# Experts' stage of a layer kernel: three buffers for the weight loads, the first product by halves, and the low part of U on VectorE

## The chip, the cores and the metric

The kernel runs on one core of a Trainium2 chip, in one launch. The metric is the device time of one execution in microseconds (us), less is better. Engines are named as the profile names them: PE (TensorE, matmuls), PEld (its weight loads), DVE (VectorE), ACT (ScalarE), POOL (GpSimd), SP (SyncE, which only issues DMAs here). SPq is the queue of SP.

## The reference

One layer on 1024 tokens of 1024 channels: a mixer sublayer (state-space scan and convolution, joined by an output projection), then a retrieval sublayer, and a last norm. The change lies in the retrieval sublayer. Every token chooses, for each of 8 heads, the 16 best of 16384 experts; an expert is a row of `u_tab` and a row of `v_tab`:

```python
def block(args):
    xb, eb, gb = args
    act = jax.nn.gelu(jnp.einsum("pd,ped->pe", xb, u_tab[eb]), approximate=False)
    return jnp.einsum("pe,ped->pd", gb * act, v_tab[eb])
...
x = x + mod[:, 5, None, :] * peer(modulate(rms_norm(x, norm2_w[i]), ...), ...)
...
return rms_norm(x, final_norm_w)
```

All of it is float32. A product that must be exact to float32 is made of three: each operand is split into a high part (a copy in the type fp32r) and a low part (the rest), and low x high, high x low and high x high are summed.

## The kernel before, in words

Tokens come in 8 blocks of 128. Before the experts' stage the kernel has normed the tokens (`h2T`, channels on partitions), chosen the experts of the first seven blocks and, for the first five (`ND`), written a matrix of gates to DRAM (`g_dram`). The experts' stage does two things side by side.

**The dense blocks.** For the first five blocks all 16384 experts are computed, 128 at a time, with TensorE. `In` (one object per 128 experts, 128 in all) is the first product: `load` brings 128 columns of U (512 KB, tile `u`) and, for every second object, a tile of gates `gm`; `split` makes the high part `uh` (ACT) and the low part `ul` (POOL) of U by `hi_lo`; `mm` calls `multiply_u`, 48 matmuls of 320 columns into two PSUM tiles `pa` (one per half of the 640 tokens; the pool has three); `post` applies the activation into `ga` (ACT); `weigh` multiplies `ga` by the gates (DVE) and makes the high part `wh` (ACT); `low` makes the low part `wl` (DVE). `Out` (256 objects) is half of the columns of the second product for 128 experts: `load` brings 128 x 512 of V (256 KB, tile `v`), `split` makes `vh` (ACT) and `vl` (DVE), `mm` issues 15 matmuls of 512 columns into five PSUM tiles `pv`, which sum over a group of 8 experts' blocks; `sum` adds them to the output in `h2T` (DVE) at the end of a group.

**The gathered blocks.** For the last three blocks the rows of U and V that each token chose are gathered: `gathered()` yields one step per row and token block. A step issues an indirect DMA of 512 KB on POOL's queue (`ask`, tile `gr`, a ring of `NGB` = 5 buffers, three asked ahead) and runs one multiply-and-sum on DVE (`scalar_tensor_tensor`). `finish(z, a)` is the end of such a block: the residual and the last norm, with loads of `x1_dram` and of a gate row into tiles of the same ring. `h2`, the tokens of a gathered block, is reloaded between blocks. `advance` interleaves these steps with the dense work: about 2.8 steps in each `In.mm` and 1.7 in each `Out.mm`, counted by `IN_US` and `OUT_US`. The choice of the last block's experts (`choosing`) is interleaved in the same place during the first groups.

**The order.** `seq` lists the objects: 8 In, then for each group 8 Out of the first columns, one In of the next group, 8 Out of the second columns, seven In. Each engine runs its instructions in the order in which the loop at the end emits them, and a queue of DMAs stops at a DMA that has to wait for its buffer. The loop emits, for object n: the load of object n+2, the split of object n+1, `weigh` of the object before if it was an In, the product of n with its share of gather steps, `low` of the object before, and `post` of n:

```python
for n, x in enumerate(seq):
    if n + 2 < len(seq):
        seq[n + 2].load()
    if n + 1 < len(seq):
        seq[n + 1].split()
    before = seq[n - 1] if n and isinstance(seq[n - 1], In) else None
    if before:
        before.weigh()
    x.mm()
    if before:
        before.low()
    x.post()
```

The tiles `u`, `uh`, `ul`, `v`, `vh`, `vl` and `gm` have two buffers each. In the last group `post` of the first Out objects also loads the residual and scales the sums (POOL), for the last norm of the dense blocks. The rows of the trace name the lines: L60 is the low part made by `hi_lo`, L59 its high part; L985 the first product; L1415 to L1417 the second; L1275 the gather; L1297 and L1309 the gathered multiply-and-sums with U and with V; L1380 the activation, L1384 `weigh`, L1386 `wh`, L1390 `wl`, L1401 V's load, L971 U's.

Of the kernel before, what the change touches and what calls it, by code (L numbers as in the profile page):

```python
# [18 lines left out]
P = 128  # L19
# [18 lines left out]
ND = 5                   # token blocks whose experts go through dense products; the others gather theirs  # L38
TD = ND * P
TH = TD // 2  # L40
NS = 7                   # token blocks whose experts are chosen before the products
NGB = 5                  # rows of gathered experts on chip
IN_US, OUT_US = 18, 11    # shares of the gather steps beside 128 experts' first product and half of their second
GE = 8                   # blocks of 128 experts between two sums into the output

# The pairs of ranks (i, j) that can be among the top ones: (i + 1)(j + 1) <= 16; those of the upper half have
# (i + 1)(j + 1) <= 8. Pieces are (i0, i1, j0, j1); sums stand in lexicographic order, numbers of experts with the first 20 ahead.
# [15 lines left out]
def mm3(nc, out, a, b, n, start=True, stop=True):  # L63
    """out += sum_k a[k].T @ b[k] in float32 accuracy; a, b give (hi, lo) pairs of a k."""
# [7 lines left out]
def layer_kernel(ctx, tc, A, dbg=None):  # L72
# [8 lines left out]
    # ------------------------------------------------------------------ constants  # L81
# [9 lines left out]
    def rsqrt(dst, src, scale, n):  # L91
        """dst = 1 / sqrt(src * scale + eps) on a small tile, with one Newton step."""
# [15 lines left out]
    row_dram = dram.tile([1, D], F32, name="row_dram")          # gate of the second sublayer  # L108
# [3 lines left out]
    g_dram = dram.tile([ND, 2, P, P, P // 2], F32, name="g_dram")   # gates: [token block, half, second key, first key, token]  # L112
# [32 lines left out]
    # chunks of w_in_t: 0-3 z, 4-7 x, 8-9 B, 10-11 C, 12-15 GLU value, 16-19 GLU gate, 20 dt  # L145
# [14 lines left out]
    def modulate(j):  # L160
        """h1 of the tokens or of the context in [channel, token] layout, split."""
# [9 lines left out]
    # ------------------------------------------------------------------ modulation, norm 1  # L171
    with ExitStack() as st:
# [22 lines left out]
        # sums of squares of the tokens from the transposed tensors  # L195
# [17 lines left out]
        # rows of scale and shift for both conditions, then as columns  # L213
# [747 lines left out]
    mix.close()  # L961
    dbg("h2T", h2T)

    # ------------------------------------------------------------------ what the dense experts need first
    late = ExitStack()
    e1 = e2 = hh2 = hl2 = None
    U = {}
# [599 lines left out]
```

## Time and profile before

| | |
|---|---|
| median of 3 runs | 3207.91 us (3204.24 to 3208.45) |
| profiled execution, span from the first to the last instruction | 3212.8 us |
| PE busy | 2880.9 us, 90% of the span |
| DVE busy | 2693.3 us, 84% |
| POOL busy | 2002.0 us, 62% |
| ACT busy | 1002.9 us, 31% |
| gathers, queue q0 | 402.70 MB, 35.5% of the 16 DMA engines' time |
| other loads, queue q1 | 315.72 MB, 28.6% |

The profiled execution's own time is its span; no time outside the span is given for it. The profile is that of one execution on the chip: busy time is the time in which an engine ran an instruction, idle time before an instruction is put down to what ended it ("<-"). In groups of instructions a mean is that of one instruction in ns. Names are the program's tiles, out<-in. The matrix engine's matmuls are pipelined: the time from one start to the next is what one costs.

### The profile page before, as it was taken

The page shows a single profiled execution, that of the slowest core. Times are in us where ns is not written, and L with a number is a line of the kernel's source. Part 1 is how long each engine was busy: PE and PEld are TensorE (multiplying, and loading weights), DVE is VectorE, ACT ScalarE, POOL GpSimd, SP SyncE. Part 2 cuts the span into 40 slices and gives each one's busy share as a digit, 9 for nine tenths or more (in the row PEclk, how much of TensorE's full clock was granted, in tenths as well). Part 3 has the DMA queues.
Part 4 walks back from the last instruction along what each step waited for, and adds up shares of the span by engine and source line. Part 5 has one row for each costly group of instructions (what it writes and reads, how often), then busy time and mean ns, then how long its engine had stood idle before and what let it go on. Part 6 is the DMA issues. An engine that isn't in the chain of part 4 may idle for free.

```text
span 3212.8 us, 41810 instructions
## 1 busy us (share of the span) xinstructions
PE 2880.9 (90%) x14905; PEld 2383.1 (74%) x14905; DVE 2693.3 (84%) x4828; ACT 1002.9 (31%) x1584; POOL 2002.0 (62%) x1478
## 2 busy tenths in 40 slices
PE   7999777998888768988999999999999899999996
PEld 4777676754555558877788788888888788888884
DVE  5897888559999997889898887888898888888896
ACT  3224323324555552322222222222222222222222
POOL 0222455316666777777677676776687677777773
PEclk8999998999999879999999999999999999999998
DMA  6111454341212237877888888899889889889883
GB/s 203 59 40 40 127 160 147 99 164 60 85 80 105 105 125 264 314 262 268 298 276 306 303 303 309 315 313 323 302 310 325 303 299 331 308 303 319 303 312 109
DMA packets 334113, 721.09 MB, mean 224 GB/s; under 512 B 24512, under 2 KB 167120, under 8 KB 332624
## 3 DMA queue, kind: packets, MB, share of 16 engines
q0 software_dynamic: 110592, 402.70, 35.5%
q1 hardware_dynamic: 223312, 315.72, 28.6%
q8 instruction: 117, 1.92, 0.2%
q14 instruction: 92, 0.75, 0.1%
HBM read 656.99 MB, written 61.35 MB: 224 GB/s over the span
## 4 chain that ended last, share of the span: by engine, by line
DVE 31%; DMA 19%; PE 18%; issue 16%; POOL 12%; ACT 2%; SPq 0%; POOLq 0%; DVEq 0%; ACTq 0%
POOL gr L1275 7%; DMA gr<-in_peer_v_dram,idx 6%; DMA v<-in_peer_v_dram 5%; DMA gr<-in_peer_u_dram,idx 5%; PE pa L985 4%; PE pa L67 4%; DVE gr L1297 3%; DVE o L1206 2%; POOL ul L60 2%; DVE ob L1198 2%; DVE cfm L407 2%; DVE oh L1076 2%; PE pv L1416 2%; PE pq L946 2%; PE pv L1417 2%
## 5 line engine op out<-in xcount | busy, mean ns | idle before, releaser
L1275 POOL DMA_INDIRECT gr<-in_peer_u_dram,idx x384 | 521.3, 1358 | 216.2 <-DVE gr L1297 130.5
L1275 POOL DMA_INDIRECT gr<-in_peer_v_dram,idx x384 | 504.6, 1314 | 212.4 <-DVE h2T L1309 124.2
L1309 DVE SCALAR_TENSOR_TENSOR h2T<-gr,wv,h2T 128x1024 f32<-128x1024 f32 x381 | 535.5, 1405 | 61.5 <-DMA gr<-in_peer_v_dram,idx 55.1
L1297 DVE SCALAR_TENSOR_TENSOR gr<-gr,h2T 128x1024 f32<-128x1024 f32 x384 | 514.3, 1367 | 73.2 <-DMA gr<-in_peer_u_dram,idx 62.2
L1416 PE MATMUL pv<-vl,wh 128*128 128x512 f32 x1280 | 523.6, 409 | 56.2 <-DVE vl L60 53.9
L1415 PE MATMUL pv<-vh,wl 128*128 128x512 f32 x1280 | 515.5, 403 | 15.2 <-ACT vh L59 15.0
L1417 PE MATMUL pv<-vh,wh 128*128 128x512 f32 x1280 | 512.5, 400 | 0.0
L985 PE MATMUL pa<-hl,uh 128*128 128x320 f32 x2000 | 329.7, 315 | 52.6 <-ACT ga L1380 48.6
L60 POOL TENSOR_TENSOR ul<-u,uh 128x1024 fp32r<-128x1024 f32 x128 | 332.9, 2601 | 66.7 <-ACT uh L59 58.1
L59 ACT ACTIVATE vh<-v 128x512 fp32r<-128x512 f32 x256 | 161.1, 630 | 643.1 <-DMA v<-in_peer_v_dram 522.0
L1416 PEld LDWEIGHTS pv<-vl,wh 128*128 128x128 f32 x1280 | 244.8, 191 | 148.4 <-DVE vl L60 91.9
L985 PEld LDWEIGHTS pa<-hl,uh 128*128 128x128 f32 x2000 | 305.2, 191 | 65.2 <-ACT ga L1380 58.2
L985 PE MATMUL pa<-hh,ul 128*128 128x320 f32 x2000 | 322.2, 315 | 4.5 <-POOL ul L60 4.5
L60 DVE TENSOR_TENSOR vl<-v,vh 128x512 fp32r<-128x512 f32 x256 | 186.4, 728 | 157.0 <-ACT vh L59 152.0
L985 PE MATMUL pa<-hh,uh 128*128 128x320 f32 x2000 | 313.6, 309 | 0.0
L985 PEld LDWEIGHTS pa<-hh,ul 128*128 128x128 f32 x2000 | 307.3, 193 | 5.3 <-POOL ul L60 5.3
L1415 PEld LDWEIGHTS pv<-vh,wl 128*128 128x128 f32 x1280 | 244.7, 191 | 84.0 <-ACT vh L59 26.2
L985 PEld LDWEIGHTS pa<-hh,uh 128*128 128x128 f32 x2000 | 298.4, 188 | 0.0
L1417 PEld LDWEIGHTS pv<-vh,wh 128*128 128x128 f32 x1280 | 244.7, 191 | 54.5
L1200 POOL TENSOR_TENSOR o<-ob,tr 128x512 f32<-128x512 bf16 x160 | 216.1, 1352 | 108.9 <-DVE ob L1198 99.7
L1184 PEld LDWEIGHTS pg<-o,o 128*128 128x128 f32 x1280 | 173.5, 207 | 131.1 <-issue 62.3
L1386 ACT ACTIVATE wh<-ga 128x640 fp32r<-128x640 f32 x128 | 94.8, 740 | 543.5 <-DVE ga L1384 527.3
(351 smaller groups left out, 4661.9 us busy)
## 6 DMA issues: line engine op xcount, KB each, us to landing
u<-in_peer_ut_dram SPq DMA_DIRECT2D x128, 512.0 KB
v<-in_peer_v_dram SPq DMA_DIRECT2D x256, 256.0 KB
g_dram<-stg SPq DMA_DIRECT2D x10, 4096.0 KB
gm<-g_dram SPq DMA_DIRECT2D x64, 640.0 KB
ld<-in_ada_w_dram SPq DMA_DIRECT2D x24, 512.0 KB
w<-in_w_in_t_dram SPq DMA_DIRECT2D x21, 512.0 KB
raw<-in_ada_w_dram SPq DMA_DIRECT2D x8, 1024.0 KB
h2T<-in_wqT_dram SPq DMA_DIRECT2D x16, 512.0 KB
```

The source lines that it names most:

```text
L59: nc.scalar.activation(hi, src, AF.Copy)
L60: (eng or nc.vector).tensor_tensor(lo, src, hi.bitcast(F32), op=OP.subtract)
L67: nc.tensor.matmul(out, a(k)[i], b(k)[j], start=start and t == 0 and k == 0, stop=stop and t == 2 and k == n - 1)
L985: nc.tensor.matmul(pa[half], x[:, k], y[:, k, half * TH:half * TH + TH], start=t == 0 and k == 0, stop=t == 2 and k == KD - 1)
L1184: nc.tensor.matmul(pg[:, j], o2[:, j], o1[:, j], start=True, stop=True)
L1200: nc.gpsimd.tensor_tensor(o2.rearrange("p t j -> p j t"), ob, tr[:, 1, None, ts].to_broadcast([P, P, 4]), op=OP.mult)
L1275: nc.gpsimd.indirect_dma_start(out=g, out_offset=None, in_=A[t], in_offset=bass.IndirectOffsetOnAxis(ap=idx[:, b, e:e + 1], axis=0))
L1297: nc.vector.scalar_tensor_tensor(g, g, 1.0, h2, op0=OP.mult, op1=OP.mult, accum_out=act[:, e:e + 1])
L1309: nc.vector.scalar_tensor_tensor(ac, g, wv[:, e:e + 1], ac, op0=OP.mult, op1=OP.add)
L1415: nc.tensor.matmul(Out.pv[t], wl[:, sl], self.vh, start=i == 0, stop=False)
L1416: nc.tensor.matmul(Out.pv[t], wh[:, sl], self.vl, start=False, stop=False)
L1417: nc.tensor.matmul(Out.pv[t], wh[:, sl], self.vh, start=False, stop=i == GE - 1)
```

## The change

The diff, without comments and lines that only moved:

```diff
+NU, NV = 3, 3
...
 def load_u(e):
-    u = e2.tile([P, KD, P], F32, name="u")
+    u = spare if e > 3 and e % 3 == 2 else e2.tile([P, KD, P], F32, name="u")
     nc.sync.dma_start(u, A["peer_ut"][e])
     return u

 def split_u(u):
     uh = e2.tile([P, KD, P], F32R, name="uh")
     ul = e2.tile([P, KD, P], F32R, name="ul")
-    hi_lo(nc, uh, ul, u, nc.gpsimd)
+    nc.scalar.activation(uh, u, AF.Copy)
+    return uh, ul, u
+
+def lower_u(uh, ul, u):
+    nc.vector.tensor_tensor(ul, u, uh.bitcast(F32), op=OP.subtract)
     return uh, ul

 def multiply_u(uh, ul, pa):
-    for t, (x, y) in enumerate(((uh, hl2), (ul, hh2), (uh, hh2))):
-        for half in range(2):
+    for half in range(2):
+        for t, (x, y) in enumerate(((uh, hl2), (ul, hh2), (uh, hh2))):
             for k in range(KD):
...
-h2, ac, fw = (h2T[:, ND + i] for i in range(3))
-nc.sync.dma_start(fw, A["final_norm_w"].partition_broadcast(P))
+h2, ac, spare = (h2T[:, ND + i] for i in range(3))
+spare_w, spare = spare, spare.rearrange("p (k t) -> p k t", t=P)

 def finish(z, a):
     xt = gp.tile([P, D], F32, name="gr")
-    nc.sync.dma_start(xt, x1_dram[z * P:(z + 1) * P, :])
+    nc.gpsimd.dma_start(xt, x1_dram[z * P:(z + 1) * P, :])
     rw = gp.tile([P, D], F32, name="gr")
-    nc.sync.dma_start(rw, row_dram[0].partition_broadcast(P))
+    nc.gpsimd.dma_start(rw, row_dram[0].partition_broadcast(P))
...
     nc.vector.tensor_tensor(a, a, rw, op=OP.mult)
+    nc.gpsimd.dma_start(rw, A["final_norm_w"].partition_broadcast(P))
...
-    nc.vector.scalar_tensor_tensor(a, a, sf[:, 1:2], fw, op0=OP.mult, op1=OP.mult)
+    nc.vector.scalar_tensor_tensor(a, a, sf[:, 1:2], rw, op0=OP.mult, op1=OP.mult)
...
 if b + 1 < NT - ND:
-    nc.sync.dma_start(h2, h2n_dram[(b + 1) * P:(b + 2) * P, :])
+    nc.gpsimd.dma_start(h2, h2n_dram[(b + 1) * P:(b + 2) * P, :])
...
 class Out:
     def load(self):
-        self.v = ep2.tile([P, 512], F32, name="v")
+        self.v = ep2.tile([P, 512], F32, name="v", bufs=NV)
...
     def post(self):
         nc.sync.dma_start(Out.rw, row_dram[0].partition_broadcast(P))
+        nc.sync.dma_start(spare_w, A["final_norm_w"].partition_broadcast(P))
...
-for x in seq[:2]:
-    x.load()
+passed = {In: 0, Out: 0}
+queues = {(kind, what): iter([x for x in seq if isinstance(x, kind)]) for kind, what in
+          ((In, "load"), (In, "split"), (In, "lower"), (In, "gate"), (Out, "load"), (Out, "split"))}
+begun = dict.fromkeys(queues, 0)
+def begin(kind, what, far):
+    while begun[kind, what] < passed[kind] + far:
+        begun[kind, what] += 1
+        x = next(queues[kind, what], None)
+        if x:
+            getattr(x, what)()
+begin(In, "load", NU + 1)
+begin(Out, "load", NV)
 for n, x in enumerate(seq):
-    if n + 2 < len(seq):
-        seq[n + 2].load()
-    if n + 1 < len(seq):
-        seq[n + 1].split()
+    begin(In, "split", 2)
+    begin(Out, "split", 2)
+    begin(Out, "load", NV + 2)
     before = seq[n - 1] if n and isinstance(seq[n - 1], In) else None
     if before:
         before.weigh()
+    passed[type(x)] += 1
+    begin(In, "gate", 2)
     x.mm()
     if before:
         before.low()
+    begin(In, "lower", 1)
+    begin(In, "load", NU + 1)
     x.post()
```

The load of the gate tile `gm` is a method of its own now (`gate`), and `lower` calls `lower_u`. Loads, splits and low parts are no longer counted in objects of `seq` but in objects of their own kind: V three ahead of its split, whatever stands between; U into the next of three buffers once that buffer's `uh` and `ul` are made. The third buffer of U is the slice of `h2T` that held the last norm's weights (`spare`); those are loaded once for each gathered block, and in the last group for the dense ones. The 128 instructions that make `ul` move from POOL to DVE; the number of matmuls is the same.

TensorE, one first product in the middle of the stage, before (`pa_9245` and `pa_9246` are its two halves):

```order
L985 MATMUL pa_9245<-hl2_8582,uh_9160 128x320 x8
L985 MATMUL pa_9246<-hl2_8582,uh_9160 128x320 x8
L985 MATMUL pa_9245<-hh2_8581,ul_9161 128x320 x8
L985 MATMUL pa_9246<-hh2_8581,ul_9161 128x320 x8
L985 MATMUL pa_9245<-hh2_8581,uh_9160 128x320 x8
L985 MATMUL pa_9246<-hh2_8581,uh_9160 128x320 x8
```

And after:

```order
L990 MATMUL pa_10161<-hl2_8582,uh_9830 128x320 x8
L990 MATMUL pa_10161<-hh2_8581,ul_9831 128x320 x8
L990 MATMUL pa_10161<-hh2_8581,uh_9830 128x320 x8
L990 MATMUL pa_10162<-hl2_8582,uh_9830 128x320 x8
L990 MATMUL pa_10162<-hh2_8581,ul_9831 128x320 x8
L990 MATMUL pa_10162<-hh2_8581,uh_9830 128x320 x8
```

The second half now follows the whole of the first, and `ul` is read from the ninth matmul on, before from the seventeenth.

VectorE, one step of a run of first products, before (L1297 is a gathered multiply-and-sum):

```order
L1292 TENSOR_TENSOR wv<-wv,gates 128x32
L1384 TENSOR_TENSOR ga<-ga,gm 128x640
L1297 SCALAR_TENSOR_TENSOR gr,act<-gr,h2T 128x1024 x3
L1390 TENSOR_TENSOR wl<-ga,wh 128x640
L1384 TENSOR_TENSOR ga<-ga,gm 128x640
```

And after (L1303 and L1315 are the gathered multiply-and-sums):

```order
L1396 TENSOR_TENSOR ga<-ga,gm 128x640
L1315 SCALAR_TENSOR_TENSOR h2T<-gr,wv,h2T 128x1024
L1303 SCALAR_TENSOR_TENSOR gr,act<-gr,h2T 128x1024 x2
L1402 TENSOR_TENSOR wl<-ga,wh 128x640
L982 TENSOR_TENSOR ul<-u,uh 128x1024
L1396 TENSOR_TENSOR ga<-ga,gm 128x640
```

The low part `ul` of the next first product stands last in the step, behind three gathered rows and `wl`.

SP's queue at the end of a gathered block, before:

```order
L1401 DMA v<-in_peer_v_dram 128x512 x3
L1249 DMA gr<-x_dram 128x1024
L1251 DMA gr<-row_dram 128x1024
L1401 DMA v<-in_peer_v_dram 128x512 x5
L1264 DMA out_dram<-h2T 128x1024
```

The same loads after, on POOL's queue among the gathers:

```order
L1281 DMA gr<-in_peer_u_dram,idx 128x1024 x4
L1254 DMA gr<-x_dram 128x1024
L1256 DMA gr<-row_dram 128x1024
L1281 DMA gr<-in_peer_u_dram,idx 128x1024 x5
L1260 DMA gr<-in_final_norm_w_dram 128x1024
```

The two loads leave V's queue for the gathers' own, and one load of the last norm's weights joins them.

## Rows read from the trace of the kernel before

**Rows 1.** Stages: length; busy PE, PEld, DVE, ACT, POOL; PEclk, DMA share, GB/s.

```profile
1202.00:1734.00 532.00, 478.25 (x2501) 418.41 (x2501) 450.64 (x795) 139.65 (x224) 384.47 (x293) 0.95 0.81 281
1734.00:3064.00 1330.00, 1273.02 (x6864) 1119.07 (x6863) 1119.43 (x1290) 335.10 (x547) 965.81 (x637) 0.99 0.89 311
2073.40:2101.40 28.00, 28.00 (x122) 22.60 (x121) 20.98 (x36) 7.51 (x11) 19.73 (x15) 1.00 0.97 348
2101.40:2152.40 51.00, 50.20 (x338) 49.30 (x338) 46.55 (x59) 14.51 (x26) 43.56 (x27) 1.00 0.88 302
```

**Rows 2.** Timeline of PE, starts of products: start (us), length (us), instruction.

```profile
1202.29 0.47 PE L985 MATMUL pv<-hl,uh 128*128 128x320 f32 x1
...
1733.66 0.31 PE L985 MATMUL pa<-hl,uh 128*128 128x320 f32 x1
...
2066.40 2.51 PE L985 MATMUL pa<-hl,uh 128*128 128x320 f32 x16
...
2073.44 0.39 PE L1415 MATMUL pv<-vh,wl 128*128 128x512 f32 x1
...
3063.91 0.31 PE L985 MATMUL pa<-hl,uh 128*128 128x320 f32 x1
```

**Rows 3.** Waits of PE, 1202 to 3064 us: total us, times, longest us.

```profile
PE pa L985 <- ACT ga L1380: 46.4, 27, 8.8
PE pv L1416 <- DVE vl L60: 42.2, 62, 4.4
PE pv L1415 <- ACT vh L59: 11.1, 14, 4.1
PE pa L985 <- POOL ul L60: 4.5, 3, 2.8
PE pa L985 <- ACT uh L59: 3.7, 1, 3.7
```

**Rows 4.** Timeline of PE around a hole: [idle before, what ended it].

```profile
1931.77 0.80 PE L1415 MATMUL pv<-vh,wl 128*128 128x512 f32 x1 [4.12 <-ACT vh L59]
...
1933.09 0.63 PE L1417 MATMUL pv<-vh,wh 128*128 128x512 f32 x1
```

**Rows 5.** Waits of ACT, 1202 to 3064 us.

```profile
ACT vh L59 <- DMA v<-in_peer_v_dram: 510.1, 138, 11.5
```

**Rows 6.** Chain that ended last, two loads of V: start us, us.

```profile
1314.69 6.13 DMA v<-in_peer_v_dram
...
1422.49 12.08 DMA v<-in_peer_v_dram
```

**Rows 7.** Groups, 1202 to 3064 us: busy us, mean ns, idle us before and its cause.

```profile
L1297 DVE SCALAR_TENSOR_TENSOR gr<-gr,h2T 128x1024 f32<-128x1024 f32 x384 | 514.3, 1367 | 73.2 <-DMA gr<-in_peer_u_dram,idx 62.2 <-issue 10.3
L1309 DVE SCALAR_TENSOR_TENSOR h2T<-gr,wv,h2T 128x1024 f32<-128x1024 f32 x353 | 488.0, 1383 | 58.9 <-DMA gr<-in_peer_v_dram,idx 53.2 <-issue 0.3
L1390 DVE TENSOR_TENSOR wl<-ga,wh 128x640 fp32r<-128x640 f32 x121 | 160.8, 1329 | 1.6 <-DMA gm<-g_dram 0.8 <-ACT wh L1386 0.8
...
L60 POOL TENSOR_TENSOR ul<-u,uh 128x1024 fp32r<-128x1024 f32 x121 | 313.1, 2588 | 66.6 <-ACT uh L59 58.1 <-PE pv L1417 6.1 <-issue 0.7
```

**Rows 8.** Timeline of DVE and POOL, single instructions.

```profile
1908.71 1.22 DVE L1254 TENSOR_TENSOR h2T<-h2T,gr 128x1024 f32<-128x1024 f32 x1
1909.85 1.21 DVE L1297 SCALAR_TENSOR_TENSOR gr<-gr,h2T 128x1024 f32<-128x1024 f32 x1
...
2111.40 2.41 POOL L60 TENSOR_TENSOR ul<-u,uh 128x1024 fp32r<-128x1024 f32 x1
2111.82 3.08 DVE L1297 SCALAR_TENSOR_TENSOR gr<-gr,h2T 128x1024 f32<-128x1024 f32 x1 [0.52 <-DMA gr<-in_peer_u_dram,idx]
...
2121.68 0.81 DVE L1390 TENSOR_TENSOR wl<-ga,wh 128x640 fp32r<-128x640 f32 x1
```

**Rows 9.** Groups, whole trace: the activation after the first product.

```profile
L1380 ACT ACTIVATE ga<-pa 128x320 f32<-128x320 f32 x252 | 103.3, 431 | 196.7 <-PE pa L985 188.7 <-issue 7.7
```

**Rows 10.** Timeline of POOL, an indirect DMA beside a DVE instruction.

```profile
1915.69 1.68 POOL L1275 DMA_INDIRECT gr<-in_peer_u_dram,idx  x1 [1.34 <-DVE gr L1297]
```

More of the change, by code (lines that the diff above doesn't have):

```diff
@@ L993, in prepare @@
             yield
-        uh, ul = split_u(U.pop(0))
+        uh, ul = lower_u(*split_u(U.pop(0)))
         pa = done[0] = [psA.tile([P, TH], F32, name="pa") for _ in range(2)]
@@ L1003, in prepare @@
         U[2] = load_u(2)
-        U[1] = split_u(U[1])
+        U[1] = lower_u(*split_u(U[1]))
         U[3] = load_u(3)
@@ L1360, in load, with gate @@
                     U[self.e] = load_u(self.e)
+            def gate(self):
                 if self.e % 2 == 0:
@@ L1368, in split, with lower @@
                     U[self.e] = split_u(U[self.e])
+            def lower(self):
+                if self.e > 3:
+                    U[self.e] = lower_u(*U[self.e])
             def mm(self):
@@ L1444, in close @@
                 if t < 2:
-                    nc.gpsimd.tensor_tensor(x, a, fw[:, self.cs], op=OP.mult)
+                    nc.gpsimd.tensor_tensor(x, a, spare_w[:, self.cs], op=OP.mult)
             def post(self):
@@ L1472, in layer_kernel @@
             if e > 1:
-                U[e] = split_u(U[e])
+                U[e] = lower_u(*split_u(U[e]))
             done[e] = multiply_u(*U.pop(e), early[2 * e - 2:2 * e])
-        U[3] = split_u(U[3])
-        for x in seq[:2]:
-            x.load()
+        U[3] = lower_u(*split_u(U[3]))
+        passed = {In: 0, Out: 0}
[10 more added lines that the diff above has]
+        begin(Out, "load", NV)
         for n, x in enumerate(seq):
-            if n + 2 < len(seq):
-                seq[n + 2].load()
-            if n + 1 < len(seq):
-                seq[n + 1].split()
+            begin(In, "split", 2)
+            begin(Out, "split", 2)
+            begin(Out, "load", NV + 2)
             before = seq[n - 1] if n and isinstance(seq[n - 1], In) else None
@@ L1502, in layer_kernel @@
             else:
-                nc.vector.scalar_tensor_tensor(acc[:, t], acc[:, t], rs[:, t:t + 1], fw, op0=OP.mult, op1=OP.mult)
+                nc.vector.scalar_tensor_tensor(acc[:, t], acc[:, t], rs[:, t:t + 1], spare_w, op0=OP.mult, op1=OP.mult)
             nc.sync.dma_start(A["out"][t * P:(t + 1) * P, :], acc[:, t])
```

## The prediction

> **What bounds the kernel now.** I read the table of stages first, then where TensorE's groups begin, then who TensorE waits for, and last how long single VectorE and GpSimd instructions take. The experts' stage runs from 1202 us to the end. In the table [rows 1] the reader is to see that TensorE is the fullest engine in it (478 of 532 us, then 1273 of 1330), VectorE second (451 and 1119), and that the 16 DMA engines are 0.81 and 0.89 full. So the stage is a TensorE stream with holes, and its floor can be read from places without holes [rows 2]: a first product (In) takes 2073.44 - 2066.40 = 7.04 us for 48 matmuls, and the eight Out (halves of a second product) from 2073.4 us on, with TensorE busy throughout, 28.00 us [rows 1], 3.50 each. A group of eight In and sixteen Out has a floor of 8 x 7.04 + 16 x 3.50 = 112.3 us. The starts of the first, fifth and sixteenth group [rows 2] give (1733.66 - 1202.29) / 4 = 132.8 us for the four groups that also choose experts and (3063.91 - 1733.66) / 11 = 120.9 us for the next eleven. Over the fifteen groups 1861.6 - 15 x 112.3 = 177 us are lost. That is all that the change can win in them.
>
> The waits of TensorE in that stretch [rows 3] sum to 46.4 + 42.2 + 11.1 + 4.5 + 3.7 = 107.9 us. The other 69 us are not waits: after a hole of 4.12 us a 512-column matmul is 0.63 us long instead of 0.39 for a while, the lower of the clock's two levels (1.2 against 2.4 GHz); the mean granted clock is 0.95 and 0.99 of full in the two stretches [rows 1, 2, 4]. A microsecond of wait has so cost 177 / 107.9 = 1.64 us, and I count what goes at that rate.
>
> **The change, part by part.**
>
> *Loads of V with three buffers, 42.2 + 11.1 us.* TensorE waits in Out for `vl` and `vh`, and ScalarE, which makes `vh`, waits 510 us for V's DMA [rows 5]. With two buffers the load of half j+2 can be issued once `vl` of j is made, during product j-1 or so, and ScalarE wants it less than two products (7 us) later. A load takes 6.13 us in an ordinary place of the chain and 12.08 us in the worst [rows 6], so the ordinary one barely fits and each slower one makes a hole. With three buffers it is issued three products (10.5 us) ahead: the ordinary load then has 4 us to spare, the worst one is late by 1.6. The wait cannot go entirely, since `vl` also stands behind gathers on VectorE, whose rows wait 62.2 + 53.2 us for their own DMA [rows 7]. Bounds: half of it, all of it. I take three quarters, 40 us, nearer to the upper end because the ordinary load has clear room.
>
> *First product by halves, 46.4 us.* The wait of `pa` for `ga` is a wait for a PSUM buffer: three buffers, and before the change the second half of a product started 8 matmuls (1.17 us) in, so the buffer had to be read out by the activation by then. By halves the second half starts 24 matmuls (3.52 us) in, 2.35 us later. The row has 27 waits; the longest is 8.8, the mean 1.72 [rows 3]. If each shrinks by 2.35 us, all but a few long ones vanish; the few long ones (VectorE late with choosing) keep their excess. I leave 9 us, so 37 go. Bounds: half, all.
>
> *Low half of U on VectorE.* POOL loses 121 instructions of 2.59 us in this stretch, 313 us [rows 7]. VectorE gains as many; the price of one is that of a 128x1024 addition of two SBUF operands on VectorE, 1.22 us, 1.14 to the next start [rows 8], so 138 us. Against this stands what GpSimd's instruction does to VectorE today: a multiply-and-sum of a gathered row takes 1.21 us alone and 3.08 us when it begins beside GpSimd's `ul` [rows 8]. In the means it shows as 1.367, 1.383 and 1.329 us where 1.21, 1.21 and 0.81 are the plain times [rows 7, 8]; 384 x 0.157 + 353 x 0.173 + 121 x 0.52 = 184 us. So VectorE gives back more than it takes, some 45 us in 1862. The Trainium skill (Perfetto Trace Analysis, Identifying the Most-Contended Engine) takes occupancy as a fair measure of VectorE's load and would relieve the fullest engine first; by that rule the 138 us are a loss and nothing comes back, and the sum is that of the second rival below. I go by rows 8: part of that occupancy is an instruction held up. What POOL gains (17% of its time) lets gathers be issued sooner, and nothing waits for POOL's `ul` (4.5 us) any more. The 3.7 us for `uh` go too: U is loaded up to three products ahead.
>
> What is late next is `ul` itself. In the order of VectorE it now stands last in a step, behind three gathers and `wl`, and with halves TensorE wants it after 8 matmuls (1.17 us) rather than 16. From the start of an In product: activation of the one before 0.43 [rows 9] and its signals (0.75 together, an estimate), then `ga` 0.81, three gathers 3.42, `wl` 0.81, `ul` 1.14, so ready at 6.9 us; wanted at 7.04 + 1.17 = 8.2. A gather waits 115.4 / 737 = 0.16 us on average [rows 7], 0.44 us per In step of 2.8 gathers, so the mean step fits with 0.9 us to spare and a slow gather does not. I put 12 us there, a tenth of all the gather waits. Bounds: 0 and 25.
>
> *Loads moved to the GpSimd queue.* Two loads of h2, and three per gathered block's end (the last norm's weights are the new one), eleven in all. An indirect DMA occupies POOL for 1.68 us beside VectorE work [rows 10], so some 11 x 1.7 = 19 us, if a plain load costs as much there, of an engine that is now 17% emptier; I cost it at nothing, covered by POOL's own slack before each gather. If that cover were gone, the eleven would delay one gather each, inside the 0 to 25 above. The SP queue no longer stops for VectorE at these places.
>
> *Sum.* Waits: -40 - 37 - 8.2 + 12 = -73 us, at 1.64 a gain of 120 us. What lies before 1202 us has four `ul` moved, and the end after the last group has its own waits that the change leaves; both count zero, within a few us. The profiled execution spans 3212.8 us, and no time around the span is given for it; it lies 4.9 us above the median of the runs, 3207.9. So 3212.8 - 120 - 4.9 = **3088 us**. With the poor bounds (27 + 23 + 8 - 25 = 33, gain 54) 3154; with all bounds good the floor, 3031.
>
> **Rivals.**
>
> *The transfers become the bound.* In an Out run on the floor the DMA engines are 0.97 full at 348 GB/s [rows 1]. At the floor the late groups would need 311 x 120.9 / 112.3 = 335 GB/s, at my forecast about 324; that is below 348, so I hold against it. But if 311 GB/s is what a mean over long stretches can hold, only the first four groups win, 532 x (1 - 281 / 311) = 51 us: 3157 us.
>
> *VectorE becomes the bound (the slower side).* Suppose the long instructions of rows 7 are not GpSimd's doing and nothing is given back. In the In run from 2101.4 us VectorE is busy 46.55 us for seven steps [rows 1], 6.65 each; with `ul` 7.79, with the gather waits 8.23, over TensorE's 7.04. Against 51.0 / 7 = 7.29 per In now that is +0.94 x 120 = 113 us; the V loads would still give 40 x 1.64 = 66, so the kernel loses 47: 3255 us. It decides at an In step of 7.29 + 66 / 120 = 7.84 us. For it: VectorE is the second fullest engine and gets work. Against it: the pair in rows 8 overlaps in time exactly, and 184 us of VectorE's busy time fit POOL's 313. This is what the Trainium skill's rule on the most-contended engine, above, would expect.
>
> *The holes only move.* Gathers pace VectorE and the new buffers fill without use: 3208 us, within 6. Against it, a run of Out on the floor exists today [rows 1].
>
> *Everything goes.* All 177 us: 3031 us. Against it, the gather waits stay.
>
> **How the numbers follow.** Forecast 0.62, transfers 0.15, everything 0.10, VectorE 0.08, holes move 0.05. A measurement of this kernel can tell about 0.2% (6.4 us) from no change. Faster: 0.62 + 0.15 + 0.10 = 0.87; same 0.05; slower 0.08. The range reaches from 3040, a little short of the floor, to 3165, which takes in the poor bounds and the transfers' case.
>
> **What would show it.** Right: groups of about 116 us late and 121 to 123 early by the starts of their first product; TensorE's waits for `vl` and `vh` below 15 us and for `ga` below 12 in the fifteen groups; no `ul` on POOL, gathered-row instructions at 1.2 to 1.25 us; a new wait of `pa` for VectorE's `ul` of 5 to 25 us; DMA 0.92 full. Wrong: a wait of `pa` for `ul` over 60 us with VectorE over 95% busy (the VectorE rival); holes filled by waits on gathers with the DMA share at 0.89 and V's loads landing after 9 us or more (transfers); gathered-row instructions still at 1.37 us, which would refute the give-back.

## The result and the profile after

The changed kernel takes **3134.45 us** (median of 4 runs, 3129.54 to 3139.47), the kernel before 3206.07 (4 runs); the ratio is **0.9773**, with a 95% interval of 0.9757 to 0.9790. That is 72 us less; 120 were forecast. The profiled execution spans 3127.7 us, 85 less than the 3212.8 of before. The gap between 85 and 72 is that the one stands 6.7 us above its kernel's median and the other 6.7 below; the working below is in profile time.

The table of stages of the kernel after: length; busy time of PE, PEld, DVE, ACT and POOL with counts; PEclk, DMA share, GB/s. The stretches are the first four groups, the next eleven, and the end.

```profile
1202.77:1728.42 525.65, 471.29 (x2498) 420.50 (x2498) 433.92 (x835) 142.45 (x225) 319.48 (x263) 0.94 0.84 289
1728.42:2985.87 1257.45, 1241.76 (x6866) 1114.91 (x6865) 1085.14 (x1381) 341.90 (x546) 761.99 (x555) 1.00 0.94 329
2985.87:3127.70 141.83, 112.66 (x577) 97.73 (x575) 103.50 (x104) 37.03 (x68) 67.41 (x40) 0.90 0.57 197
```

The bounds of the stretches are the starts of first products in the timeline of PE after, which answer to [rows 2]:

```profile
1202.77 2.04 PE L990 MATMUL pv<-hl,uh 128*128 128x320 f32 x8
...
1728.40 1.19 PE L990 MATMUL pa<-hl,uh 128*128 128x320 f32 x7
...
2985.86 1.33 PE L990 MATMUL pa<-hl,uh 128*128 128x320 f32 x8
```

A late group takes (2985.86 - 1728.40) / 11 = **114.3 us**, where it took 120.9, 2.0 over the floor of 112.3: 73 us. An early group takes (1728.40 - 1202.77) / 4 = **131.4 us**, where it took 132.8: 6 us in all. The end gives 7 (141.8 after 148.9), and what lies before the stage is the same.

Waits of PE after, first in the four early groups, then in the eleven late ones (total us, times, longest us):

```profile
PE pa L990 <- DVE ul L982: 30.4, 6, 10.1
PE pv L1428 <- DVE vl L61: 13.4, 5, 5.5
PE pa L990 <- ACT uh L978: 8.3, 1, 8.3
...
PE pv L1428 <- DVE vl L61: 7.7, 9, 1.6
PE pa L990 <- DVE ul L982: 7.0, 10, 1.3
```

The same stretches in the kernel before, whose sums over both are in [rows 3]:

```profile
PE pa L985 <- ACT ga L1380: 24.7, 7, 8.8
PE pv L1416 <- DVE vl L60: 23.3, 22, 4.4
...
PE pa L985 <- ACT ga L1380: 21.7, 20, 3.7
PE pv L1416 <- DVE vl L60: 18.9, 40, 2.9
```

Late, the waits fell from 55.7 us (with the rows for vh, uh and two small ones) to 15.5 (with one of 0.8), and 40 us of wait were worth 73 us. Early, they were 53.5 us and are 54.3, all rows taken: ga and half of vl went, ul and uh came. The groups on VectorE, 1202 to 2990 us, answer to [rows 7]; the releasers of [rows 5] on ACT in the fifteen groups follow:

```profile
L1303 DVE SCALAR_TENSOR_TENSOR gr<-gr,h2T 128x1024 f32<-128x1024 f32 x384 | 463.9, 1235 | 57.5 <-DMA gr<-in_peer_u_dram,idx 52.8 <-issue 3.3 <-DMA h2T<-h2n_dram 1.0
L1315 DVE SCALAR_TENSOR_TENSOR h2T<-gr,wv,h2T 128x1024 f32<-128x1024 f32 x356 | 457.4, 1285 | 34.9 <-DMA gr<-in_peer_v_dram,idx 28.6
L982 DVE TENSOR_TENSOR ul<-u,uh 128x1024 fp32r<-128x1024 f32 x82 | 100.0, 1221 | 0.0
L1402 DVE TENSOR_TENSOR wl<-ga,wh 128x640 fp32r<-128x640 f32 x121 | 99.1, 819 | 1.6 <-ACT wh L1398 1.6
...
ACT vh L60 <- PE pv L1429: 617.4, 221, 10.1
ACT vh L60 <- DMA v<-in_peer_v_dram: 9.8, 3, 3.5
```

The gathered rows' instructions and wl are back near their plain times, and ScalarE, which waited 510 us for V's DMA [rows 5], waits 9.8: it now waits for TensorE.

**Where the early holes are.** Two kinds are left. At the start it is SP's queue. The timeline of SP, DVE and PE there:

```profile
1211.33 9.19 SPq L1413 DMA_DIRECT2D v<-in_peer_v_dram  x5
1220.58 1.69 SPq L1371 DMA_DIRECT2D gm<-g_dram  x2
...
1228.25 0.82 DVE L1396 TENSOR_TENSOR ga<-ga,gm 128x640 f32<-128x640 f32 x1 [8.09 <-DMA gm<-g_dram]
...
1233.86 2.50 PE L990 MATMUL pa<-hl,uh 128*128 128x320 f32 x8 [8.35 <-ACT uh L978]
1246.41 2.50 PE L990 MATMUL pa<-hh,ul 128*128 128x320 f32 x8 [10.05 <-DVE ul L982]
```

Five loads of V, the last two waiting for buffers, stand ahead of the first gates. After that it is VectorE. Here is a step of the third group on DVE, from ga to ul, with the matmuls that wait for it:

```profile
1501.06 0.81 DVE L1396 TENSOR_TENSOR ga<-ga,gm 128x640 f32<-128x640 f32 x1
1501.79 0.78 DVE L1069 TENSOR_REDUCE ef<-oh 128x8 f32<-128x160 f32 x2
...
1507.02 1.22 DVE L1303 SCALAR_TENSOR_TENSOR gr<-gr,h2T 128x1024 f32<-128x1024 f32 x1 [1.31 <-DMA gr<-in_peer_u_dram,idx]
1510.03 1.23 DVE L1303 SCALAR_TENSOR_TENSOR gr<-gr,h2T 128x1024 f32<-128x1024 f32 x1 [1.77 <-DMA gr<-in_peer_u_dram,idx]
1511.18 0.82 DVE L1402 TENSOR_TENSOR wl<-ga,wh 128x640 fp32r<-128x640 f32 x1
1511.91 1.22 DVE L982 TENSOR_TENSOR ul<-u,uh 128x1024 fp32r<-128x1024 f32 x1
...
1513.18 2.50 PE L990 MATMUL pa<-hh,ul 128*128 128x320 f32 x8 [4.69 <-DVE ul L982]
1515.48 2.33 PE L990 MATMUL pa<-hh,uh 128*128 128x320 f32 x8
1517.62 1.68 PE L990 MATMUL pa<-hl,uh 128*128 128x320 f32 x8
1519.14 1.04 PE L990 MATMUL pa<-hh,ul 128*128 128x320 f32 x6
```

The choice (L1069, and L1081 behind it) and two late gathers stretch the step to 12 us where 7.04 fit, and ul, last in it, is 4.69 us late. The late gathers, 1.31 and 1.77 us, are the larger part of these 5 us. The four rows of PE also show why a wait costs more than itself: eight matmuls, 1.17 us from start to start on the floor (7.04 / 6), take 2.30, 2.14 and 1.52 after the hole, 2.44 us more. The granted clock is 0.56 of full from 1513.2 to 1519.1 us, after these 4.69 us without a matmul, so most of that stretch ran at the lower level, 1.2 GHz.

### The profile page after: what moved, and what is told of

The parts are those of the page before. It is cut to its first block, busy times and chain, and to the rows that moved or that the text cites. A ratio compares the mean times of both kernels' runs of the same rounds, so it can differ in the third digit from the quotient of the medians.

```text
span 3127.7 us, 41600 instructions
## 1 busy us (share of the span) xinstructions
PE 2841.5 (91%) x14905; PEld 2381.7 (76%) x14905; DVE 2632.5 (84%) x4956; ACT 1011.7 (32%) x1584; POOL 1713.4 (55%) x1361
## 4 chain that ended last, share of the span: by engine, by line
PE 44%; DVE 29%; issue 10%; DMA 8%; POOL 6%; ACT 2%; SPq 0%; DVEq 0%; POOLq 0%; ACTq 0%
PE pa L990 18%; PE pv L1428 5%; PE pv L1429 5%; PE pv L1427 5%; POOL gr L1281 4%; DMA gr<-in_peer_u_dram,idx 4%; DVE cfm L408 3%; DVE o L1211 3%; PE pa L68 3%; DVE ob L1203 2%; PE pq L947 2%; DVE oh L1081 2%; DMA gr<-in_peer_v_dram,idx 2%; DVE gr L1303 1%; DVE h2T L1315 1%
## 5 line engine op out<-in xcount | busy, mean ns | idle before, releaser
L1281 POOL DMA_INDIRECT gr<-in_peer_v_dram,idx x384 | 537.6, 1400 | 325.5 <-DVE h2T L1315 219.1
L1428 PE MATMUL pv<-vl,wh 128*128 128x512 f32 x1280 | 513.4, 401 | 26.0 <-DVE vl L61 25.9
L1315 DVE SCALAR_TENSOR_TENSOR h2T<-gr,wv,h2T 128x1024 f32<-128x1024 f32 x381 | 495.7, 1301 | 38.3 <-DMA gr<-in_peer_v_dram,idx 31.5
L1303 DVE SCALAR_TENSOR_TENSOR gr<-gr,h2T 128x1024 f32<-128x1024 f32 x384 | 463.9, 1235 | 57.5 <-DMA gr<-in_peer_u_dram,idx 52.8
L990 PE MATMUL pa<-hh,ul 128*128 128x320 f32 x2000 | 340.3, 313 | 40.1 <-DVE ul L982 39.2
L990 PE MATMUL pa<-hl,uh 128*128 128x320 f32 x2000 | 336.8, 311 | 8.3 <-ACT uh L978 8.3
L990 PE MATMUL pa<-hh,uh 128*128 128x320 f32 x2000 | 337.6, 311 | 0.0
L990 PEld LDWEIGHTS pa<-hh,uh 128*128 128x128 f32 x2000 | 307.5, 190 | 0.0
L1392 ACT ACTIVATE ga<-pa 128x320 f32<-128x320 f32 x252 | 110.0, 438 | 594.7 <-PE pa L990 571.0
L1189 PE MATMUL pg<-o,o 128*128 128x128 f32 x1280 | 187.4, 297 | 78.8 <-DVE o L1211 53.9
```

The lines of the kernel that those rows point to most:

```text
L990: nc.tensor.matmul(pa[half], x[:, k], y[:, k, half * TH:half * TH + TH], start=t == 0 and k == 0, stop=t == 2 and k == KD - 1)
L1189: nc.tensor.matmul(pg[:, j], o2[:, j], o1[:, j], start=True, stop=True)
L1281: nc.gpsimd.indirect_dma_start(out=g, out_offset=None, in_=A[t], in_offset=bass.IndirectOffsetOnAxis(ap=idx[:, b, e:e + 1], axis=0))
L1303: nc.vector.scalar_tensor_tensor(g, g, 1.0, h2, op0=OP.mult, op1=OP.mult, accum_out=act[:, e:e + 1])
L1315: nc.vector.scalar_tensor_tensor(ac, g, wv[:, e:e + 1], ac, op0=OP.mult, op1=OP.add)
L1392: nc.scalar.activation(self.ga[:, half * TH:half * TH + TH], self.pa[half], AF.Gelu)
```

## The experiments

All kernels were timed against the kernel before in the same session. Its median was 3205.9 us in the first session (a_ul_pool, a_by_term, a_v_two, a_lower_first), 3210.8 in the second (a_start, a_choice_2, b_halves, b_ul_dve), 3213.5 in the third (a_loads, a_u_two, a_best) and 3208.9 in the last, so small differences across sessions are read from the ratios. Early and late are us per group by the starts of first products in each one's timeline; before and after are shown again for comparison.

| kernel | median us | ratio to before, 95% interval | early | late |
|---|---|---|---|---|
| before | 3206.1 | | 132.8 | 120.9 |
| after | 3134.4 | 0.9773 (0.9757 to 0.9790) | 131.4 | 114.3 |
| a_ul_pool: ul on GpSimd, behind the gathers | 3190.1 | 0.9953 (0.9932 to 0.9975) | 135.3 | 117.8 |
| a_by_term: no halves | 3117.7 | 0.9722 (0.9704 to 0.9739) | 130.2 | 113.8 |
| a_loads: the earlier loads, ul as in a_ul_pool, no halves | 3174.5 | 0.9879 (0.9860 to 0.9898) | 134.0 | 116.9 |
| b_halves: before, with halves | 3204.4 | 0.9979 (0.9964 to 0.9995) | 131.8 | 119.9 |
| b_ul_dve: before, ul on VectorE, one object ahead | 3231.2 | 1.0074 (1.0046 to 1.0101) | 133.8 | 121.1 |
| a_v_two: two buffers for V | 3166.4 | 0.9873 (0.9856 to 0.9891) | 133.0 | 116.4 |
| a_u_two: two buffers for U | 3136.5 | 0.9759 (0.9742 to 0.9777) | 130.6 | 114.7 |
| a_lower_first: ul ahead of gathers | 3115.2 | 0.9719 (0.9699 to 0.9740) | 127.3 | 114.2 |
| a_start: first loads reordered | 3137.0 | 0.9762 (0.9737 to 0.9787) | 131.4 | 115.0 |
| a_choice_2: choice at half rate | 3120.6 | 0.9722 (0.9701 to 0.9742) | 122.9 | 116.5 |
| a_best: three edits | 3109.4 | 0.9671 (0.9653 to 0.9689) | 121.8 | 116.2 |
| a_best_20_10: gathers moved | 3129.5 | 0.9750 (0.9726 to 0.9774) | 123.8 | 116.3 |

My theory from these traces (A): the loads, the freed VectorE and the halves took the late holes; early, VectorE is late with the choice, and the hole only changed its name. The rivals are in the expectations.

**ul back on GpSimd (a_ul_pool).**

```diff
 def lower_u(uh, ul, u):
-    nc.vector.tensor_tensor(ul, u, uh.bitcast(F32), op=OP.subtract)
+    nc.gpsimd.tensor_tensor(ul, u, uh.bitcast(F32), op=OP.subtract)
```

> The changed kernel with ul back on GpSimd, all else as changed. Theory A with the give-back of the prediction (GpSimd's two-operand instruction holds up VectorE's): gathered-row instructions of the eleven late groups go back from about 1.23 and 1.28 us to 1.37 us, VectorE is as busy as now or busier although 123 instructions of 1.22 us left it, and the median rises by 10 to 50 us, to 3145 to 3185. Rival C (VectorE is the engine that is short, and 148 us of ul on it cost time, above all in the first four groups): VectorE is less busy by 100 us or more, the first four groups fall below 126 us and the median falls to 3080 to 3115.

It is 56 us slower than the change, a little more than theory A's 50. TensorE's wait for ul in the fifteen groups, then the groups on DVE and POOL in its eleven late ones:

```profile
PE pa L990 <- POOL ul L982: 67.5, 44, 10.5
...
L1315 DVE SCALAR_TENSOR_TENSOR h2T<-gr,wv,h2T 128x1024 f32<-128x1024 f32 x290 | 394.8, 1361 | 32.6 <-DMA gr<-in_peer_v_dram,idx 27.0 <-DVE vl L61 0.4 <-DVE h2T L1315 0.4
L1402 DVE TENSOR_TENSOR wl<-ga,wh 128x640 fp32r<-128x640 f32 x88 | 151.5, 1722 | 0.0
...
L982 POOL TENSOR_TENSOR ul<-u,uh 128x1024 fp32r<-128x1024 f32 x59 | 155.1, 2629 | 1.1
L982 POOL TENSOR_TENSOR ul<-h2T,uh 128x1024 fp32r<-128x1024 f32 x29 | 75.0, 2585 | 0.5
```

88 instructions of 1.22 us left VectorE, 107 us, and its busy time there rose from 1085 to 1147: 169 us of stretching beside 230 us of ul on GpSimd. wl takes 1.72 us where it took 0.82. The give-back is real; here it falls on wl and ga (1.36 us on average, 0.82 in the change) more than on the gathered rows. The Trainium skill (SBUF — State Buffer, SBUF: two separate sides) says that a VectorE instruction with two SBUF inputs and a GpSimd instruction that reads SBUF share a pair of ports as an exclusive lock, and that the loser waits out the whole instruction; the trace agrees in kind, and puts 0.73 us of VectorE's time beside each us of GpSimd's. Rival C fell.

The edit does not bring back the ul of the kernel before in full. There `split` issued it ahead of the step's gathers on POOL, and TensorE waited 4.5 us for it [rows 3]; here `lower` issues it behind them, and TensorE waits 67.5 us. The 56 us are the price of ul on GpSimd in this place; how much of them is the place was not run.

**The first product in its old order (a_by_term).**

```diff
-    for half in range(2):
-        for t, (x, y) in enumerate(((uh, hl2), (ul, hh2), (uh, hh2))):
+    for t, (x, y) in enumerate(((uh, hl2), (ul, hh2), (uh, hh2))):
+        for half in range(2):
```

> The changed kernel with the first product in its old order, each of the three terms through both halves before the next term. Theory A (the halves took away the wait of pa for the activation): that wait, zero now, comes back with 30 to 45 us in the fifteen groups, while ul is wanted 8 matmuls later and its wait falls from 37.5 to 20 us or less; in sum the median rises by 10 to 50 us, to 3145 to 3185, and the late groups lengthen from 114.3 to 115.5 to 118 us. Rival E (the wait for ga was VectorE's lateness and went with the earlier loads): the wait for ga stays below 10 us and the median stays within 8 us of 3134 or falls.

It is 17 us **faster**. Its waits of PE in the fifteen groups:

```profile
PE pa L990 <- DVE ul L982: 22.0, 7, 7.8
PE pa L990 <- ACT ga L1392: 6.0, 2, 3.3
```

The wait for ga does not come back (6.0 us, not 30 to 45), and ul's falls from 37.5 to 22.0. Rival E holds: the halves cost time here.

**The earlier loads (a_loads)**: both edits above together.

> The earlier loads alone: the changed kernel with ul back on GpSimd and the first product in its old order, term by term. The halves alone gave 6 us, ul on VectorE alone cost 20. Theory I (the parts help each other: a load that is ahead makes ul ready early, and only then does it pay to free VectorE or the second half): the loads alone give 25 to 50 us, to 3160 to 3185, of 72 in all, and TensorE's waits in the fifteen groups sum to 65 to 85 us. Rival J (the loads are the whole gain, the other two parts do nothing together): 3125 to 3145, waits below 50 us.

39 us of gain, as theory I expected. But these are not the loads alone: as in a_ul_pool, ul stands behind the step's gathers on POOL, later than in the kernel before, and the wait for it rises from 4.5 us to 43.5. What the loads give with ul in its old place was not run. Waits of PE in the fifteen groups; with 18.1 more in uh, vh and ga they sum to 95, above the 65 to 85 I gave:

```profile
PE pa L990 <- POOL ul L982: 43.5, 34, 8.1
PE pv L1428 <- DVE vl L61: 33.7, 24, 4.8
```

**The halves alone (b_halves)**: the halves' loop, as in the change, in the kernel before.

> The kernel before with the first product by halves and nothing else. The prediction's term for it: the wait of pa for ga falls from 46.4 us to about 9 in the fifteen groups, and at 1.64 the median falls by 45 to 60 us, from 3206 to 3146 to 3161. Rival E (after the look at the changed kernel without the halves, 17 us faster than with them): the halves let the second half's activation go but want ul 8 matmuls sooner, so the wait moves to ul on GpSimd: that wait rises from 4.5 us to 25 or more, and the median stays between 3180 and 3215.

6 us. Waits of PE in the fifteen groups:

```profile
PE pv L1416 <- DVE vl L60: 57.9, 56, 4.7
PE pa L985 <- POOL ul L60: 22.5, 11, 6.0
...
PE pa L985 <- ACT ga L1380: 4.5, 6, 2.1
```

The wait for ga went from 46.4 to 4.5 us, better than forecast, and 18 us of it came back for ul and 16 for vl: rival E, with 22.5 us for ul a little under its 25.

**ul on VectorE alone (b_ul_dve).**

```diff
 if before:
     before.low()
+if n + 1 < len(seq) and isinstance(seq[n + 1], In) and seq[n + 1].e > 3:
+    U[seq[n + 1].e] = lower_u(*U[seq[n + 1].e])
 x.post()
```

(`split_u` and `lower_u` as in the change.)

> The kernel before with ul made on VectorE, behind wl as in the change, and nothing else. Theory A with the give-back: the gathered rows' instructions fall from 1.37 and 1.38 us to below 1.29, wl from 1.37 to 0.82 us, VectorE is not busier than the 1119 us of the eleven late groups in spite of 88 more instructions of 1.22 us, and the wait of pa for ga falls by half with it, since the ga that frees pa no longer stands behind stretched work: the median falls by 30 to 60 us, to 3146 to 3176. Rival H (only with three buffers does this pay, since V's loads are late anyway): the waits for vl and vh stay at 53 us or rise, and the median stays within 15 us of 3206.

Slower by 0.74%. The gathered rows take 1.220 and 1.283 us in its late groups and the wait for ga is gone, as theory A had it; the time is not. The waits for vl and vh do not stay at 53 us, as rival H had it, but fall to 26.0, with two buffers. What is new is the wait for ul. Waits of PE, then of ACT, in the fifteen groups, and one of the holes on DVE and PE:

```profile
PE pa L989 <- DVE ul L981: 86.1, 30, 8.0
...
ACT vh L59 <- DMA v<-in_peer_v_dram: 369.1, 92, 10.9
...
1989.79 3.07 DVE L1438 TENSOR_TENSOR h2T<-h2T,pv 128x512 f32<-128x512 f32 x5
...
1995.08 1.22 DVE L981 TENSOR_TENSOR ul<-u,uh 128x1024 fp32r<-128x1024 f32 x1
...
1996.35 3.46 PE L989 MATMUL pa<-hh,ul 128*128 128x320 f32 x16 [2.77 <-DVE ul L981]
```

All 21 late waits for ul (48.5 us), and 69.4 of the 86.1 us in all, stand at the first product that follows a run of Out; in the changed kernel none does. The edit makes ul one object of `seq` ahead, so this one stands on VectorE behind the five sums (L1438) and the gathered rows of the last Out. The change counts in objects of In and makes the same ul before the run of Out begins. So the run shows the give-back, but its 20 us are the price of another place of ul as well as of late loads (ScalarE still waits 369 us for V's DMA), and it can't tell the two apart. What ul on VectorE gives without the earlier loads stays open.

**Two buffers for V (a_v_two)**, `NU, NV = 3, 2`.

> The changed kernel with two buffers for V and its loads one less ahead. Theory A (the third buffer of V is what took the waits for vl and vh away): those waits in the fifteen groups rise from 23.1 us to 45 to 60, at 1.64 us of time for a us of wait, and the median rises by 35 to 60 us, to 3170 to 3195. Rival D (the waits went because GpSimd no longer holds up VectorE's vl, and the third buffer is spare): vl and vh stay below 30 us and the median stays within 10 us of 3134.

32 us slower, just short of theory A's 35. ScalarE waits 398.6 us for V's DMA again, where the changed kernel has 9.8: the third buffer is what took that wait away. Of the wait of TensorE that the edit brings back, 10 us are for vl and vh, now 33.3, between the two expectations, and 13 for ul (waits of PE, then of ACT, fifteen groups):

```profile
PE pa L990 <- DVE ul L982: 50.8, 21, 10.0
PE pv L1428 <- DVE vl L61: 29.1, 19, 8.2
...
ACT vh L60 <- DMA v<-in_peer_v_dram: 398.6, 117, 13.6
```

**Two buffers for U (a_u_two).**

```diff
-NU, NV = 3, 3
+NU, NV = 2, 3
...
-    u = spare if e > 3 and e % 3 == 2 else e2.tile([P, KD, P], F32, name="u")
+    u = e2.tile([P, KD, P], F32, name="u")
```

> The changed kernel with two buffers for U and its loads one less ahead. In the kernel before with ul on VectorE alone, TensorE waits 86 us for ul in the fifteen groups. Theory K (that wait comes from U's load, which with two buffers can start only when ul of the product before is made): the wait for ul rises from 37.5 us to 55 to 85, ScalarE's uh waits for U's DMA again, and the median rises by 25 to 60 us, to 3160 to 3195. Rival L (the third buffer of V did it, U's is spare): the wait stays below 45 us and the median within 8 us of 3134.

No difference (3136.5), and a wait for ul of 40.4 us: rival L. The third buffer of U is spare.

**ul ahead of the gathers (a_lower_first).**

```diff
 begin(In, "gate", 2)
+begin(In, "lower", 1)
 x.mm()
 if before:
     before.low()
-begin(In, "lower", 1)
```

> The changed kernel with one thing moved: ul of the next product stands ahead of the step's gathers on VectorE, not behind them and wl. In the changed kernel TensorE waits 37.5 us for ul in the fifteen groups, 30.4 of it in the first four, where a group still takes 131.4 us. Theory A (in the first four groups VectorE itself is late, with the choice of the last block and its chains, and whatever stands last in its order makes the hole): the wait for ul falls below 12 us, but wl, vl or ga come later, the first four groups stay at 127 us or more, the other eleven stay within 1 us of 114.3, and the median comes to 3115 to 3135 us. Rival B (the place of ul behind the gathers is the cause): the first four groups fall to about 120 us each, 45 us in all, and the median comes to 3085 to 3100.

19 us faster, at the lower edge of theory A's ranges (3115 us, early groups 127). Waits of PE, fifteen groups:

```profile
PE pv L1428 <- DVE vl L61: 34.2, 18, 5.9
PE pa L990 <- DVE ul L982: 11.0, 4, 5.2
```

26 us left ul, and 13 of them came back for vl. Late groups are unchanged.

**The first loads reordered (a_start).**

```diff
-begin(In, "load", NU + 1)
-begin(Out, "load", NV)
+begin(In, "gate", 2)
+begin(Out, "load", 2)
+begin(In, "load", NU + 3)
+bring(NS, 0)
+nc.sync.dma_start(h2, h2n_dram[:P, :])
```

> The changed kernel with the order of the first loads alone altered: the first gates gm, two V, then U of the fifth and sixth product, the first scores and the tokens h2, and only then the other V. In the changed kernel the first group takes 146.6 us (133.9 before the change) and TensorE waits 8.3 us for uh and 10.1 us for ul in it; VectorE's ga waits 8.1 us for gm there, whose load stands on SP's queue behind five V loads of which two wait for a buffer. Theory F (the earlier V loads push what the first products need to the back of SP's queue): the first group falls to 125 to 132 us, the other groups stay within a microsecond or two, and the median falls from 3134 to 3112 to 3122. Rival A (VectorE is late with the choice whatever the loads do): the hole comes back a product later as another wait for ul, the first group stays over 140 us and the median within 6 us of 3134.

(The two moved loads leave their old places.) A miss: 3137.0, the same. The uh wait of 8.3 us is gone, the first group is 141.9 us instead of 146.6, and a wait of pa for ga of 5.8 us and a longer third group (135.1) stand in its place. The order on SP's queue is what the rows at the start show, but VectorE has the next hole ready.

**The choice at half rate (a_choice_2).**

```diff
 for _ in range(n):
-    next(choice, None)
+    turns[0] += 1
+    if turns[0] % 2 == 0:
+        next(choice, None)
```

> The changed kernel with the choice of the last block's experts given out at half its rate, so that it lasts some seven groups, not some three and a half. Theory A (VectorE is late in the first groups because of the choice): groups two to four, now 126.2, 130.2 and 122.6 us, fall to 117 to 122, groups five to seven rise by at most 3 us each, and the median falls from 3134 to 3110 to 3122. Rival G (the early groups are long for another reason, their gathers or the start): groups two to four stay within 2 us of what they are, or what they lose the next three gain, and the median stays within 6 us of 3134.

Groups two to four fell to 117.5, 120.1 and 119.0 us, the first to 135.0, and the fifth and sixth rose to 123.8 and 129.1 (113.6 and 117.6 before this edit). The holes follow the choice, as theory A had it. The time does not: groups two to four lose 22.4 us and groups five to seven gain 23.4, which is what rival G had for these sums. Of the 34 us that the first four groups win 14 are kept by the medians, about what the first group wins alone (11.6).

**Three edits together (a_best)**: a_lower_first, a_by_term and a_choice_2.

> Three edits together on the changed kernel: ul ahead of the step's gathers (19 us faster alone), the first product in its old order (17 us) and the choice at half its rate (14 us). If they are independent: 3134 - 50 = 3084. Theory A (all three shift the same VectorE lateness, in part): 3090 to 3108, the wait for ul below 10 us in the fifteen groups, the waits for vl at 25 us or more now the largest; groups one to four near 122 us on average, the late ones at 114 to 116. If they stand in each other's way: 3110 or more.

3109.4 us, just above theory A's range, and the fastest kernel here: 25 us below the change by the medians, 33 by the ratios (0.0102 x 3206). Of the 50 us of the three edits alone a half to two thirds is kept. Waits of PE, fifteen groups:

```profile
PE pv L1430 <- DVE vl L61: 37.4, 23, 5.0
```

There is no wait for ul left; VectorE's lateness shows at vl.

**The gather steps moved (a_best_20_10)**: `IN_US, OUT_US = 20, 10` in a_best.

> The kernel with the three edits together (3109.4 us) and the gather steps shared out 20 to 10 between a first product and a half of the second, not 18 to 11, so about 3.1 and 1.55 steps where it was 2.8 and 1.7. There TensorE's largest wait is for vl, 37.4 us in the fifteen groups. Theory M (vl is late because VectorE's work in an Out step, some 1.7 gathered rows of 1.25 us, vl of 0.69 and its share of the sums, leaves only about 0.3 of the 3.5 us): the wait for vl falls below 25 us, ul stays below 8, and the median falls by 8 to 30 us, to 3080 to 3101. Rival N (vl is late behind gathered rows whose DMA is late, wherever they stand): the wait stays above 30 us or goes over to ul and ga, and the median stays within 8 us of 3109 or rises.

20 us slower. vl falls by 6 us and vh rises by 9.5, to 16.6 (waits of PE, fifteen groups):

```profile
PE pv L1430 <- DVE vl L61: 31.7, 15, 3.9
```

Rival N, for the place: emptier Out steps did not take the wait away. Whether late gathers are its whole cause was not isolated.

## Why the prediction was right, and where it was not

The direction and the range held. The size did not: 120 us forecast, 72 by medians, 85 between the profiles.

**The rate of 1.64 us per us of wait** held in the late groups, where it was 73 / 40 = 1.8. Over the fifteen groups the waits fell by 39 us, not by 73, and it is the waits that were mis-sized. The prediction put the 69 us beside the waits to the lower clock; the granted clock of [rows 1] accounts for some 40 of them (0.05 x 532 + 0.01 x 1330), so 1.64 is a measured ratio whose cause is shown only in part. Late groups were forecast at about 116 and measured 114.3; early ones at 121 to 123 and measured 131.4. **The step that failed is that the sum was made over the fifteen groups as one**: it holds in the eleven late groups, and gives next to nothing in the four early ones, where VectorE also chooses experts. The prediction named the choice as the cause of the longest ga waits and still took 37 of the 46 us away.

**Loads of V, -40.** vl and vh fell from 53.3 to 23.1 us, by 30. Undoing the third buffer costs 32 us of time, where the term counted 40 x 1.64 = 66. The mechanism was right for ScalarE, whose wait for V's DMA is 398.6 us with two buffers and 9.8 with three. The size was a half: with two buffers 10 of the 30 us come back, beside 13 for ul, and the other 20 went with the rest of the change. Freeing VectorE with two buffers (b_ul_dve) leaves 26.0, though there the long wait for ul may cover part of them.

**Halves, -37.** This term is wrong in sign within the change. Alone they take the wait for ga away as forecast and give it to ul and vl (6 us of gain); with the earlier loads and ul on VectorE they cost 17 us. Each of the other two parts takes the wait for ga away without the halves: 4.0 us of it are left in a_loads, none in b_ul_dve (where the later ul may cover it), 6.0 with both parts in a_by_term. I read the 46 us as the price of when a PSUM buffer is wanted; the runs point to the lateness of who releases it, ScalarE behind V's DMA and VectorE's stretched ga. Before the change ScalarE stood 497.6 us in the fifteen groups before VectorE's ga, which it needs for wh; after it 68.0.

**ul on VectorE: -184 + 138 us of its time.** Right in sum. In the eleven late groups VectorE's busy time went from 1119 to 1085 us although 107 us of ul came: 141 given back, where 184 x 11 / 15 = 135 were forecast. That the sum fits so well is in part luck: the rows with V take 1.285 us, above the 1.21 that was taken as their plain time and above the 1.2 to 1.25 that were forecast (those with U take 1.235), and ga, which the sum left out, gave back 22 us late (94.1 to 72.4). The rule of the Trainium skill (Perfetto Trace Analysis, Identifying the Most-Contended Engine) calls occupancy a fair measure of how close VectorE is to its roofline; read so, VectorE should have been busier with ul. A part of its occupancy was time in which it was held up, and here the measurement decides against the rule. What this part is worth in time is not isolated: a_ul_pool (56 us slower than the change) and b_ul_dve (20 us slower than the kernel before) both move ul to a later place in its engine's order as well.

**The new wait for ul, +12, bounds 0 and 25.** It is 37.5 us, outside the bounds: 7.0 late, near a tenth of the gather waits as argued, and 30.4 early, which I had not costed. The mean step that the estimate used, 6.9 us, holds no work of the choice; the step shown above takes 12. That 10.1 us of it come at the very start, where the V loads that begin earlier push gm, U and the scores back on SP's queue, was missed too, though a_start shows that this hole is not worth its length.

**Loads on the GpSimd queue, 0.** The trace agrees: they hold POOL for 0.55 to 0.71 us on average, and no wait of PE points to them. Moving them back was not tried.

**The rivals.** Transfers as the bound: fell, the late groups move 329 GB/s at a DMA share of 0.94, where 311 was to be the limit. VectorE as the bound: fell as a whole, since it is 0.86 busy late and pa's wait for ul is below 60 us; it describes the early groups in part, where ul stands last behind the choice. Holes only move: fell late, and is what happened early, 53.5 to 54.3 us of waits. Everything goes: nearly so late (2.0 us per group over the floor), not early.

What stays open: how much of the early holes is VectorE's time for the choice, how much its gathers that land late (33.7 us of VectorE's waits in the four groups), and how much GpSimd's own work for the choice; the runs moved them only together.

## What to carry to other kernels

Make the sum by stage: the same wait in a stage with slack on the late engine and in one without is not the same money, and there it will turn up under another name. Before a wait for a buffer is priced, look at why its releaser is late; the halves gave 6 us alone and cost 17 beside the other two parts. A run that takes one part of a change by itself must leave every other instruction where it was: three of the runs here (a_ul_pool, a_loads, b_ul_dve) also moved ul in its engine's order, and so price two things at once. When work moves from an engine that holds another up, look at the other's instruction times, not at its busy share.

## What the runs showed of the hardware

GpSimd's two-operand instruction stretches gathered multiply-and-sums and plain two-operand instructions of VectorE alike: 230 us of ul on GpSimd lengthened VectorE's work by 169 us in a_ul_pool, and which of them pay depends on what stands beside it (wl takes 1.72 us instead of 0.82 there; before the change the gathered rows paid too, 1.37 instead of 1.21). A plain DMA issued on GpSimd takes 0.55 to 0.71 us of it on average, an indirect one 1.36 to 1.40. The DMA engines hold 329 GB/s over 1257 us, with gathers and weight loads together.
